# The second layer's modulation: from matmuls beside the first mixer to VectorE multiply-adds beside the dense channel mixer

## The chip, the cores and the metric

The kernel runs on one core of a Trainium2 chip. The metric is the time of one execution in device microseconds (us); the time before is the median of three runs. One more execution was recorded by the hardware profiler. TensorE is called PE, its weight loads PEld, VectorE DVE, ScalarE ACT, GpSimd POOL and SyncE, which issues the DMAs, SP.

## What is computed

Two layers of a hybrid backbone over 256 context and 256 latent tokens of width 1024. Each layer has a token mixer (four head groups between one input and one output projection) and a channel mixer: a dense SwiGLU in layer 0, eight experts with the best two of them in layer 1. Each layer's shifts, scales and gates, its modulation, are six vectors of 1024 for the latent tokens (from c) and six for the context tokens (from c_ctx):

```python
for l in range(DEPTH):                       # DEPTH = 2, D_MODEL = 1024, 256 latent + 256 context tokens
    ctx_out = l < DEPTH - 1
    mod_l = (jax.nn.silu(c) @ ada_w[l] + ada_b[l])[:, None, :]       # ada_w[l]: 1024 x 6144
    mod_c = jax.nn.silu(c_ctx) @ ada_w[l] + ada_b[l]
    sh1, sc1, g1, sh2, sc2, g2 = jnp.split(mod_l, 6, axis=-1)
    csh1, csc1, cg1, csh2, csc2, cg2 = jnp.split(mod_c, 6, axis=-1)
    hl = modulate(rmsnorm(xl, norm_mix[l]), sh1, sc1)
    hc = modulate(rmsnorm(xc, norm_mix[l]), csh1, csc1)
    ...
    yl = jnp.concatenate([ya_l, yb_l, yc_l, yd_l], axis=-1) @ w_out[l]
    xl = xl + g1 * yl
    hl = modulate(rmsnorm(xl, norm_ffn[l]), sh2, sc2)
    if l % 2 == 0:
        xl = xl + g2 * swiglu(hl, ffn_w13[l // 2], ffn_w2[l // 2])
    else:
        xl = xl + g2 * moe_ffn(hl, moe_router[l // 2], moe_router_b[l // 2], moe_w13[l // 2], moe_w2[l // 2])
    if ctx_out:
        ...                                  # the context stream, with cg1, csh2, csc2, cg2
```

In layer 1 the context stream ends with the token mixer, so only sh1 and sc1 are used of its context modulation. All arithmetic is float32; large products are made of a high and a low part of each operand.

## The kernel before

The stages follow one another: setup, layer 0's modulation and first normalisation (`first_h`), the first mixer (`mixer(0, True)`, then `w_out`), normalisation (`make_h`), the dense channel mixer (`ffn`), the second mixer (`mixer(1, False)`), and the experts (`moe`). Within a stage a scheduler at build time orders each engine's instructions by priority and simulated readiness; the order on every engine is fixed when the kernel runs.

**The modulation.** `ada` (line 317) makes 1024 columns of the modulation for both token kinds. The 1024 rows of `ada_w` come in eight loads of 128 x 1024 floats (512 KB, line 335) into four buffers `adaw`. For every second row block, four matmuls (line 347) multiply them by `stat`, whose two used columns are silu(c) and silu(c_ctx): 32-column weights, 512 columns, one quarter of the PSUM bank's partitions each, summed over the row blocks. ScalarE copies the bank to `adar` (line 354), four small matmuls with the constant `sel` (line 358) turn the rows into columns, and DVE adds the bias into `mod[l]` (line 363). For the last group of layer 1 two more matmuls of 512 columns (line 371) and two DVE additions (line 375) spread the channel mixer's gate over all partitions, as `g2row`, which the experts use. There are six groups in a layer. Groups 1 and 0 of layer 0 run alone in `first_h`; the other ten are steps of a generator that runs beside the first mixer.

**Beside.** `beside` (line 378) keeps a generator and a rate, one for each of two phases of the mixer. `tick` (line 388) is called after each block of matmuls of the main work and runs as many steps as the rate says. A step's instructions go behind the latest instruction of the main work on their engine (`issue_after(anchor(...))`). `finish` (line 398) runs what is left. `self.made` is the last DVE instruction of the main work at a tick; DVE instructions of helpers, and the low halves of weights, don't count for it.

**The dense mixer.** `ffn` (line 301) goes through 22 blocks of 128 hidden columns in three parts (8, 8, 6). For each pair of blocks it loads the value and the gate weights (1024 x 256 each, in two loads of 512 KB into three raw buffers), ScalarE makes the high half (line 209), DVE the low half (line 210) of each 128 x 512 piece, and PE makes four banks of 24 matmuls (lines 526 to 528, for the first block 569 to 571). ScalarE takes silu of the gate (line 1323), DVE multiplies (line 1325), ScalarE and DVE split the product (lines 1328, 1329). Then `w2` follows in four quarters with two banks each, and DVE adds the gated result to the residual `xT` (line 1343). The stage's PSUM pool has seven banks A and one bank C; only A is used in it.

## Time and profile before

| | |
|---|---|
| median of three runs | 2014.39 us (2011.48 to 2016.26) |
| profiled execution | 2016.45 us, of which the span from the first to the last instruction is 2014.7 us |
| PE busy | 1876.2 us (93%), mean granted clock 0.962 of full speed |
| PEld, DVE, ACT, POOL busy | 1235.0, 918.4, 767.2, 85.3 us |
| DMA | 474.73 MB, mean 236 GB/s |

The profile is one execution. A busy time counts each moment once in which an engine has an instruction; PE's matmuls are pipelined and their ends are modelled, so neighbouring matmuls overlap in it. A float32 matmul may show as two records. In a timeline, consecutive instructions of one line are merged: the number behind the x counts them. "Idle before" names what ended an engine's idle time. DMA is the mean busy share of the core's 16 DMA engines.

### The profile page before, as it was taken

To read this page: it belongs to the slowest core of one execution; us is meant where nothing else is said; L and a number is where in the kernel's file an instruction comes from. 1 tells how busy PE (TensorE), PEld (TensorE's weight loads), DVE (VectorE), ACT (ScalarE), POOL (GpSimd) and SP (SyncE) were. 2 spreads that over 40 slices of the span, in tenths; PEclk is the share of its full clock that TensorE was granted. 3 is DMA by queue.
4 is the path that set the end of the run, shared out by engine and by line. 5 is a ranking of instruction groups with operands and counts; after the bars stand their busy time and mean duration, and the time that the engine had idled before them with its cause. 6 is when DMAs were issued, how large, how long until landed. Compare 5 with 4: busy or idle time off the path is not lost.

```text
span 2014.7 us, 26293 instructions
## 1 busy us (share of the span) xinstructions
PE 1876.2 (93%) x10051; PEld 1235.0 (61%) x10051; DVE 918.4 (46%) x1678; ACT 767.2 (38%) x1331; POOL 85.3 (4%) x121
## 2 busy tenths in 40 slices
PE   6999999989999999888988999789999989899988
PEld 3777455678888888667686886454454444444443
DVE  3556334453433434675567965333324333333323
ACT  3745433253223233654547854232322222323221
POOL 0210111000000000210100000000000000000000
PEclk8999899989999999888998989999999989999999
DMA  8543356412323233331045969999999989999997
GB/s 276 181 136 110 126 193 204 152 63 95 96 93 96 92 97 92 102 85 48 1 166 201 363 225 380 405 408 409 401 376 349 410 321 380 409 401 372 409 405 300
DMA packets 190958, 474.73 MB, mean 236 GB/s; under 512 B 18596, under 2 KB 81768, under 8 KB 190824
## 3 DMA queue, kind: packets, MB, share of 16 engines
q1 hardware_dynamic: 190456, 472.76, 64.2%
q8 instruction: 81, 1.33, 0.3%
q14 instruction: 53, 0.43, 0.1%
q10 hardware_dynamic: 368, 0.21, 0.0%
HBM read 471.88 MB, written 1.05 MB: 235 GB/s over the span
## 4 chain that ended last, share of the span: by engine, by line
PE 63%; DMA 5%; DVE 5%; ACT 3%; issue 2%; DVEq 0%; SPq 0%; ACTq 0%
PE bankA L1572 16%; PE bankA L528 7%; PE bankA L527 7%; PE bankA L526 7%; PE bankA L1567 6%; PE bankA L1568 5%; PE bankA L1566 5%; DMA w<-in_moe_w_dram 5%; DVE wl L210 2%; ACT wh L209 1%; PE bankA L1531 1%; PE bankA L1602 1%; PE bankA L835 1%; PE bankB L874 1%; PE bankA L1714 1%
## 5 line engine op out<-in xcount | busy, mean ns | idle before, releaser
L210 DVE TENSOR_TENSOR wl<-w,wh 128x1024 fp32r<-128x1024 f32 x222 | 263.9, 1222 | 257.8 <-ACT wh L209 245.7
L209 ACT ACTIVATE wh<-w 128x1024 fp32r<-128x1024 f32 x222 | 225.7, 1053 | 156.7 <-DMA w<-in_moe_w_dram 126.7
L1572 PE MATMUL bankA<-w,xl 128*32 128x256 f32 (+3 forms) x1784 | 228.4, 452 | 15.0 <-DMA w<-in_moe_w_dram 15.0
L1572 PEld LDWEIGHTS bankA<-w,xl 128*32 128x32 f32 (+1 forms) x1784 | 83.7, 124 | 134.3 <-issue 96.5
L1567 PE MATMUL bankA<-wl,xe 128*128 128x512 f32 x336 | 140.7, 419 | 19.2 <-DVE wl L210 19.2
L1566 PE MATMUL bankA<-wh,xe 128*128 128x512 f32 x336 | 129.0, 425 | 14.8 <-ACT wh L209 14.4
L1568 PE MATMUL bankA<-wh,xe 128*128 128x512 f32 x336 | 136.5, 406 | 0.0
L1572 PE MATMUL bankA<-w,ut 128*32 128x256 f32 (+1 forms) x792 | 116.4, 490 | 0.8 <-DMA w<-in_moe_w_dram 0.8
L1650 ACT ACTIVATE sg<-bankA 128x512 f32<-128x512 f32 (+2 forms) x45 | 23.1, 533 | 196.6 <-PE bankA L1572 159.1
L1566 PEld LDWEIGHTS bankA<-wh,xe 128*128 128x128 f32 x336 | 61.7, 194 | 54.4 <-ACT wh L209 28.8
L1567 PEld LDWEIGHTS bankA<-wl,xe 128*128 128x128 f32 x336 | 65.9, 196 | 44.0 <-DVE wl L210 29.7
L1567 PE MATMUL bankA<-wl,uh 128*128 128x512 f32 x168 | 68.8, 409 | 9.4 <-DVE wl L210 9.4
L1653 DVE TENSOR_TENSOR sg<-bankA,sg 128x512 f32<-128x512 f32 (+2 forms) x45 | 27.0, 612 | 108.7 <-PE bankA L1572 89.0
L1572 PEld LDWEIGHTS bankA<-w,ut 128*32 128x32 f32 (+1 forms) x792 | 36.6, 122 | 63.9 <-issue 56.5
L1568 PEld LDWEIGHTS bankA<-wh,xe 128*128 128x128 f32 x336 | 66.0, 196 | 13.9
L528 PE MATMUL bankA<-uh,w2l 128*128 128x512 f32 x176 | 70.2, 399 | 0.0
L528 PE MATMUL bankA<-hh,wgl 128*128 128x512 f32 x176 | 70.2, 399 | 0.0
L527 PE MATMUL bankA<-hl,wgh 128*128 128x512 f32 x176 | 69.3, 394 | 0.0
L527 PE MATMUL bankA<-ul,w2h 128*128 128x512 f32 x176 | 69.3, 394 | 0.0
L526 PE MATMUL bankA<-uh,w2h 128*128 128x512 f32 x176 | 69.0, 392 | 0.0
L526 PE MATMUL bankA<-hh,wgh 128*128 128x512 f32 x176 | 69.0, 392 | 0.0
L347 PE MATMUL bankC<-adaw,stat 128*32 128x512 f32 x352 | 67.3, 617 | 1.5 <-DMA adaw<-in_ada_w_dram 1.5
(489 smaller groups left out, 3679.1 us busy)
## 6 DMA issues: line engine op xcount, KB each, us to landing
w<-in_moe_w_dram SPq DMA_DIRECT2D x286, 1024.0 KB, 10.1
adaw<-in_ada_w_dram SPq DMA_DIRECT2D x96, 512.0 KB, 4.8
xT<-in_moe_w_dram SPq DMA_DIRECT2D x47, 1024.0 KB, 9.2
wa<-in_ffn_w_dram SPq DMA_DIRECT2D x22, 512.0 KB
wg<-in_ffn_w_dram SPq DMA_DIRECT2D x22, 512.0 KB, 3.5
w<-in_ffn_w_dram SPq DMA_DIRECT2D x20, 512.0 KB, 3.4
wo<-in_w_out_dram SPq DMA_DIRECT2D x12, 512.0 KB, 3.5
wU<-in_w_in_dram SPq DMA_DIRECT2D x4, 512.0 KB
```

The costliest lines, as they stand in the source:

```text
L209: nc.scalar.activation(h, src, AF.Copy)
L210: ins = nc.vector.tensor_tensor(lo[:, q:q + m], src, h.bitcast(F32), op=OP.subtract)
L347: mark(nc.tensor.matmul(b[32 * q:32 * q + 32], lhsT=self.stat[:, j], rhs=rs[j][:, h * 512:(h + 1) * 512], start=(i == 1), stop=(i == 7)))
L526: t.matmul(out, lhsT=whi, rhs=hhi, start=start, stop=False)
L527: t.matmul(out, lhsT=whi, rhs=hlo, start=False, stop=False)
L528: t.matmul(out, lhsT=wlo, rhs=hhi, start=False, stop=stop)
L1566: t.matmul(b, lhsT=x[0], rhs=hi[:, c], start=start, stop=False)
L1567: t.matmul(b, lhsT=x[0], rhs=lo[:, c], start=False, stop=False)
L1568: t.matmul(b, lhsT=x[1], rhs=hi[:, c], start=False, stop=stop)
L1572: t.matmul(out[0][n * s:n * s + n, 0:h], lhsT=x, rhs=w[:, s * h:(s + 1) * h], start=start, stop=stop)
L1650: nc.scalar.activation(g[:, 0:h], b[:, 0:h], AF.Silu)
L1653: V.tensor_tensor(g[:, 0:h], b[:, 0:h], g[:, 0:h], op=OP.mult)
```

## The change

Layer 1's six groups leave the generator beside the first mixer. Layer 0's four remaining groups keep it, with matmuls in batches of eight instead of four, a lag of one step instead of three, and half the rate. A new generator, `ada_vec`, makes layer 1's modulation beside the dense mixer, in twelve units of 512 columns. A unit loads eight blocks of 128 x 512 (256 KB each) into six buffers; DVE multiplies the first block by silu(c), one scalar for each partition, and adds the seven others times their scalars (`scalar_tensor_tensor`); units 0 to 3 do so for c and c_ctx, the others for c alone. DVE then transposes the sum in blocks of 32 x 32 and sums the 32 columns of each block; four matmuls with a new constant `fold` (four stacked 32 x 32 identities) add the four partition groups into a bank C, and DVE adds the bias. For the last two units one matmul of 512 columns with `ones` each spreads the gate for `g2row`. `ffn` gets ticks after its gate and value banks (24 matmuls each) and, at 0.7, after its w2 banks. The setup keeps silu(c) in a tile `sl` of its own.

```diff
--- before.py
+++ after.py
@@ -33,7 +33,7 @@
 BEYOND = ((0, 160, 128), (1, 128, 128), (2, 64, 128), (3, 64, 64), (4, 64, 64), (5, 64, 64), (6, 32, 64), (7, 128, 128))
 
 CONST_COLS = {
-    "base": [("ident", 128), ("ones", 128), ("sel", 4)],
+    "base": [("ident", 128), ("ones", 128), ("sel", 4), ("fold", 32)],
     "mix": [("mask_f", 128), ("mask_b", 128), ("swa_m0", 128), ("swa_m1", 128), ("sel_i", 64), ("sel_f", 64)],
     "rope": [("mla_c", 128), ("mla_s", 128), ("swa_c", 256), ("swa_s", 256)],
     "moe": [("utri", 128), ("iota", 320), ("idx8", 8), ("rev8", 8), ("tri8", 64)],
@@ -85,6 +85,7 @@
         put(n + "_c", cs)
         put(n + "_s", sn)
 
+    put("fold", np.tile(np.eye(32), (4, 1)))
     put("sel", np.stack([(p % 32 == m) & (p // 32 % 2 == h) for h in range(2) for m in range(2)], 1))
     si, sf = np.zeros((128, 64)), np.zeros((128, 64))
     for h in range(4):
@@ -237,14 +238,14 @@
 
         b = self.bank()
         nc.tensor.transpose(b[:, 0:16], p0, self.ident[0:16, 0:16])
-        sl = self.mp.tile([128, 16], F32, name="sl")
+        sl = self.sl = self.cp.tile([128, 16], F32, name="sl")
         self.stat = self.mp.tile([128, 8, 32], F32, name="stat")
         nc.gpsimd.memset(self.stat, 0.0)
         nc.scalar.activation(sl, b[:, 0:16], AF.Exp, scale=-1.0)
         nc.vector.tensor_scalar(sl, sl, 1.0, None, op0=OP.add)
         nc.vector.reciprocal(sl, sl)
-        nc.vector.tensor_tensor(self.stat[:, :, 0:2], sl.rearrange("p (s k) -> p k s", s=2),
-                                b[:, 0:16].rearrange("p (s k) -> p k s", s=2), op=OP.mult)
+        nc.vector.tensor_tensor(sl, sl, b[:, 0:16], op=OP.mult)
+        nc.vector.tensor_copy(self.stat[:, :, 0:2], sl.rearrange("p (s k) -> p k s", s=2))
         self.p2 = self.T2("p2", shape=(128, 128))
         nc.gpsimd.memset(self.p2, 1.0)
         self.load_x()
@@ -338,14 +339,15 @@
             if not lag:
                 load(k)
             i = k - lag
-            if i > 0 and i % 2:
-                if i == 1:
+            if i > 0 and i % 4 == 3 or not lag and i % 2:
+                if b is None:
                     b = self.bank(tag)
                 with own(nc.tensor):
-                    for q in range(4):
-                        j, h = i - 1 + q // 2, q % 2
-                        mark(nc.tensor.matmul(b[32 * q:32 * q + 32], lhsT=self.stat[:, j], rhs=rs[j][:, h * 512:(h + 1) * 512],
-                                              start=(i == 1), stop=(i == 7)))
+                    for f in range(i // 4 * 4 if lag else i - 1, i, 2):
+                        for q in range(4):
+                            j, h = f + q // 2, q % 2
+                            mark(nc.tensor.matmul(b[32 * q:32 * q + 32], lhsT=self.stat[:, j],
+                                                  rhs=rs[j][:, h * 512:(h + 1) * 512], start=(f == 0), stop=(f == 6)))
             if lag and k < 8:
                 load(k)
             yield
@@ -364,16 +366,57 @@
                                          b[:, 0:16].rearrange("p (j h m) -> p j h m", h=2, m=2),
                                          self.pc1[:, o:o + 8].rearrange("p (h j) -> p j h", h=2).unsqueeze(3)
                                          .to_broadcast([128, 4, 2, 2]), op=OP.add))
-        if l == 1 and g == 5:
-
-            for h in range(2):
-                with own(nc.tensor):
-                    mark(nc.tensor.matmul(b, lhsT=self.C("sel")[:, 2 * h:2 * h + 1].to_broadcast([128, 128]), rhs=row,
-                                          start=True, stop=True))
-                s = self.g2row[:, h * 512:(h + 1) * 512]
-                with own(nc.vector):
-                    mark(nc.vector.tensor_tensor(s, b, s, op=OP.add))
-        yield
+        yield
+
+    def ada_vec(self, l, n, mk, segs=(0, 1), lag=0):
+
+
+        nc = self.nc
+        acc = [mk("adaacc") if m in segs else None for m in range(2)]
+        src = self.I["ada_w"][l, :, n * 512:(n + 1) * 512].rearrange("(k p) c -> p k c", p=128)
+        for k in range(8):
+            r = mk("adav")
+            with self.tc.issue_after(self.anchor(nc.sync)):
+                ins = nc.sync.dma_start(r, src[:, k])
+            self.aside.add(ins.ins.name)
+            for m in segs:
+                sc = self.sl[:, 8 * m + k:8 * m + k + 1]
+                a = acc[m]
+                with self.tc.issue_after(self.made):
+                    if k:
+                        ins = nc.vector.scalar_tensor_tensor(a, r, sc, a, op0=OP.mult, op1=OP.add)
+                    else:
+                        ins = nc.vector.tensor_scalar(a, r, sc, None, op0=OP.mult)
+                    self.aside.add(ins.ins.name)
+            yield
+        for _ in range(lag):
+            yield
+
+        m0, ns = segs[0], len(segs)
+        sm = mk("adasum", (128, 32))[:, 0:16 * ns].rearrange("p (m c) -> p m c", m=ns)
+        for i, m in enumerate(segs):
+            t = mk("adat")
+            with self.tc.issue_after(self.made):
+                a = nc.vector.transpose(t, acc[m])
+                b = nc.vector.tensor_reduce(sm[:, i], t.rearrange("p (b c) -> p b c", c=32), axis=AX.X, op=OP.add)
+                self.aside |= {a.ins.name, b.ins.name}
+        for _ in range(lag):
+            yield
+        last = self.anchor(nc.tensor)
+        o = l * 64 + 16 + 4 * n
+        with self.tc.issue_after(last):
+            b = self.bank("C")
+            sv = sm.rearrange("p m (j q) -> p q m j", q=4)
+            for q in range(4):
+                nc.tensor.matmul(b[32 * q:32 * q + 32, 0:4 * ns], lhsT=self.C("fold"), rhs=sv[:, q], start=True, stop=True)
+            nc.vector.tensor_tensor(self.mod[l][:, 4 * n:4 * n + 4, m0:m0 + ns],
+                                    b[:, 0:4 * ns].rearrange("p (m j) -> p j m", m=ns),
+                                    self.pc1[:, o:o + 4].unsqueeze(2).to_broadcast([128, 4, ns]), op=OP.add)
+            if l == 1 and n >= 10:
+                b = self.bank("C")
+                nc.tensor.matmul(b, lhsT=self.C("ones"), rhs=acc[0], start=True, stop=True)
+                s = self.g2row[:, (n - 10) * 512:(n - 9) * 512]
+                nc.vector.tensor_tensor(s, b, s, op=OP.add)
 
     def beside(self, gen, rate):
 
@@ -1318,6 +1361,7 @@
                         for k in range(KD):
                             self.mm3(b, hi[:, k, s], lo[:, k, s], self.hh[k], self.hl[k], k == 0, k == KD - 1)
                         bs.append(b)
+                        self.tick()
                 for j in range(2):
                     sg = fp.tile([128, NT], F32, name="sg", tag="sg", bufs=2)
                     nc.scalar.activation(sg, bs[2 + j], AF.Silu)
@@ -1344,6 +1388,7 @@
                                                        self.xT[m][:, c], op0=OP.mult, op1=OP.add)
                     if f0 == 16:
                         self.square_x(m)
+                    self.tick(0.7)
 
 
     U2 = 22
@@ -1822,8 +1867,7 @@
                 def mk(nm, sh):
                     return self.mp.tile(list(sh), F32, name=nm, tag=nm, bufs={"adaw": 4, "adar": 1}[nm])
 
-                todo = [(0, g) for g in (2, 3, 4, 5)] + [(1, g) for g in range(6)]
-                self.beside(overlap([self.ada(l, g, mk, lag=3) for l, g in todo], 10), (1.2, 2.4))
+                self.beside(overlap([self.ada(0, g, mk, lag=1) for g in (2, 3, 4, 5)], 10), (0.6, 1.2))
                 self.mixer(0, True)
                 self.ahead = 0
                 self.w_out(0, True)
@@ -1832,7 +1876,11 @@
             self.scale_mod(0, 1)
             with pool(name="ffn0", bufs=1) as fp, pool(name="ffn0s", bufs=1) as self.mp, self.psum("pffn", A=7, C=1):
                 self.make_h(0, 1, self.ffn_h(fp))
+                mk = lambda nm, sh=(128, NT): fp.tile(list(sh), F32, name=nm, tag=nm,
+                                                      bufs={"adaacc": 6, "adav": 6, "adat": 3, "adasum": 2}[nm])
+                self.beside(overlap([self.ada_vec(1, n, mk, (0, 1) if n < 4 else (0,), lag=2) for n in range(12)], 8), 1.8)
                 self.ffn(0, fp)
+                self.finish()
                 self.scale_mod(1, 0)
                 self.scale_mod(1, 1, 1)
             with pool(name="y1", **right) as yp, self.psum("pmix1", A=4, B=4):
```

## Rows read from the trace of the kernel before

**Rows 1.** The page, part 1: busy time of PE over the span.
```profile
PE 1876.2 (93%) x10051; PEld 1235.0 (61%) x10051; DVE 918.4 (46%) x1678; ACT 767.2 (38%) x1331; POOL 85.3 (4%) x121
```

**Rows 2.** The chain that ended last: start us, us, what.
```profile
427.04 2.93 PE bankA L422 x16
...
810.38 1.93 PE bankA L422 x16
```

**Rows 3.** The table of stretches: the stretch, its length, then as its head says.
```profile
core 0: us, PE busy (x) PEld busy (x) DVE busy (x) ACT busy (x) POOL busy (x), PEclk, DMA share, GB/s
...
43.00:427.00 384.00, 374.61 (x1937) 241.02 (x1937) 189.28 (x476) 166.31 (x372) 46.02 (x64) 0.97 0.48 153
...
262.00:391.00 129.00, 129.00 (x718) 69.90 (x718) 51.18 (x159) 37.95 (x113) 13.46 (x22) 1.00 0.59 193
...
445.00:534.00 89.00, 89.00 (x383) 71.31 (x382) 34.56 (x53) 32.08 (x53) 0.00 (x0) 1.00 0.30 95
445.00:800.00 355.00, 355.00 (x1523) 285.32 (x1522) 139.72 (x223) 111.96 (x186) 0.00 (x0) 1.00 0.30 92
830.00:1040.00 210.00, 193.66 (x1140) 151.85 (x1139) 132.02 (x339) 111.03 (x244) 35.55 (x44) 0.93 0.21 60
970.00:1030.00 60.00, 60.00 (x397) 46.47 (x396) 32.24 (x110) 23.62 (x71) 10.14 (x16) 1.00 0.00 1
```

**Rows 4.** Timeline of PE, 262 to 275 us: start us, us, engine, line, operation.
```profile
264.98 1.06 PE L347 MATMUL bankC<-adaw,stat 128*32 128x512 f32 x8
265.97 0.66 PE L860 MATMUL bankA<-c_base,P 128*128 128x128 f32 x4
...
270.68 1.05 PE L347 MATMUL bankC<-adaw,stat 128*32 128x512 f32 x4
271.66 0.44 PE L860 MATMUL bankA<-c_base,P 128*128 128x128 f32 x2
```

**Rows 5.** Groups by line, 262 to 391 us: operation, count, busy us, mean ns, idle before.
```profile
L347 PE MATMUL bankC<-adaw,stat 128*32 128x512 f32 x192 | 37.0, 604 | 0.0
...
L358 PE MATMUL bankC<-c_base,adar 128*128 128x4 f32 x48 | 6.0, 248 | 0.0
...
L371 PE MATMUL bankC<-adar,c_base 128*128 128x512 f32 x4 | 2.2, 624 | 0.0
```

**Rows 6.** Table of stretches for line 347 alone: PE, PEld, clock, DMA share, GB/s.
```profile
214.00:262.00 48.00, 13.53 (x64) 1.83 (x64) 0.91 0.51 168
```

**Rows 7.** Timelines of weight loads (PEld): one modulation group, one old fold.
```profile
264.98 0.16 PEld L347 LDWEIGHTS bankC<-adaw,stat 128*32 128x32 f32 x8
...
279.97 0.97 PEld L358 LDWEIGHTS bankC<-c_base,adar 128*128 128x128 f32 x8
```

**Rows 8.** Groups of DVE by line and shape, whole span: count, busy us, mean ns.
```profile
L842 DVE TENSOR_REDUCE nm<-bankA 128x1 f32<-128x512 f32 x32 | 22.1, 691 | 34.7 <-PE bankA L835 18.9 <-PE bankA L838 15.4 <-POOL P L854 0.4
...
L1068 DVE SCALAR_TENSOR_TENSOR uc<-uT,pc,uc 128x510 f32<-128x510 f32 x8 | 5.6, 742 | 0.0
...
L1065 DVE TENSOR_SCALAR uc<-uT,pc 128x512 f32<-128x512 f32 x4 | 2.3, 612 | 0.0
```

**Rows 9.** Timeline of DVE, 61 to 66 us: four multiply-adds in a row.
```profile
62.96 2.73 DVE L1068 SCALAR_TENSOR_TENSOR uc<-uT,pc,uc 128x510 f32<-128x510 f32 x4
```

**Rows 10.** Timelines of DVE and PE in the dense mixer, at the step to w2.
```profile
529.22 0.69 DVE L210 TENSOR_TENSOR w2l<-w,w2h 128x512 fp32r<-128x512 f32 x1 [0.72 <-ACT w2h L209]
...
528.99 0.40 PE L528 MATMUL bankA<-uh,w2l 128*128 128x512 f32 x1
...
533.19 0.40 PE L528 MATMUL bankA<-uh,w2l 128*128 128x512 f32 x1
```

**Rows 11.** Waits of SP's queue, 430 to 810 us: us in total, times, longest us.
```profile
SPq L182 <- DVE w2l L210: 113.7, 24, 8.0
```

**Rows 12.** DMA issues, whole span: count, KB each, median us to landing.
```profile
wg<-in_ffn_w_dram SPq DMA_DIRECT2D x22, 512.0 KB, 3.5
...
wo<-in_w_out_dram SPq DMA_DIRECT2D x8, 256.0 KB, 3.2
```

## The prediction

> **What bounds the kernel now.** I read the page first: over the whole span TensorE (PE) is busy 93% [rows 1], so the first question is whether that busy time is real work in the two stages the change touches. The chain of work that ended last gives the edges of the stages: the sums for the two norms that follow the first mixer and the dense channel mixer stand at 427 and 810 us [rows 2]. I then cut the span with the table of stretches [rows 3]. The first mixer runs from 43 to 427 us, the dense mixer from about 445 to 809, the second mixer to about 1040, the experts to the end. In the first mixer PE is idle 384 - 374.6 = 9.4 us, and in its stretch from 262 to 391 not at all, while VectorE (DVE) is busy 40% of that stretch and ScalarE 29%. In the dense mixer PE is busy all of the 355 us read there and DVE 39%. So PE sets the pace on both sides of the move, and DVE has room on average where the work is going. The experts' stage does not read a clock of its own: it starts when the second mixer ends, so what is gained before 810 us moves the end by as much.
>
> Third, PE's timeline inside the stretch from 262 to 391 [rows 4]. A group of four modulation matmuls (8 records) starts at 264.98 and the next instruction at 265.97: it holds PE for 0.99 us. Split in two (4 records each) either half also holds it for 0.98 us (270.68 to 271.66). These durations repeat, so they are occupation and not hidden waiting.
>
> **What it removes from the first mixer.** All of layer 1's modulation lies between 262 and 391 us. Its busy time by groups of instructions [rows 5]: 37.0 us in the weighted sums (192 records are 24 groups of four; at about 1.05 a piece that is 35 pieces, so 11 groups were issued as two halves), 6.0 us in the 48 records that fold the rows into columns, 2.2 us in the two broadcasts for g2row; together 45.2 us. A piece reads 0.07 longer than it holds PE (270.68 + 1.05 against 271.66), 3 us over 43 pieces; I keep 45.2 and leave that to the range. The six ScalarE copies, the DVE additions and 48 loads of 512 KB go as well; none of these ends a PE wait today, so they count as nothing here.
>
> At this place a rule speaks against the change. The table of stretches has weight loads (PEld) busy 69.9 of 129 us, 54%, between 262 and 391, and 285 of 355, 80%, in the dense mixer [rows 3]. The Trainium skill, "Perfetto Trace Analysis", section "Identifying the Most-Contended Engine", says that matmul busy time is a poor measure for TensorE and that weight-load busy time and arithmetic share show its headroom. By it the stretch would have headroom in which the 45 us lay free of charge, and the sum would begin with 0 instead of -45. I do not take it: the starts in [rows 4] show the next matmul pushed back by the whole piece.
>
> **Layer 0's four groups.** They stay on PE, at half the rate and in batches of eight matmuls. Between 214 and 262 us 64 records, eight groups of four, took 13.5 us [rows 6]; eight whole pieces at 1.05 would be 8.4, and one piece there ran at a lowered clock (the stretch's mean is 0.91), so about four were split, 4 us. Batches can save between 0 and 4.2 us; I take 3. Their 42 steps at half the rate last as long as 84 of the old 104, so they still end before the output projection ends, so nothing waits for them.
>
> **What it adds to PE in the dense mixer.** Twelve folds, each four matmuls on 32-column weights with at most 8 columns, and two broadcasts of 512 columns. No such fold is in the trace. Upper bound: the old fold, the same count with 128-column weights, 6.0 / 6 = 1.0 us each [rows 5], so 12.0. Lower: weights of 32 columns load eight in 0.16 us where the old fold's eight take 0.97 [rows 7], and one record of the old fold lasts 0.248, so 0.41 each, 4.9. I take 0.6, as the loads are those of the cheap kind and the rest that of the dear: 7.2. The broadcasts have the shape of those removed: 2.2. In a stage with no idle PE none of it is hidden: +9.4 (7.1 to 14.2). A fold also waits for its unit's reduction, with the dense matmuls queued behind it on PE; it is emitted two steps later (2 / 1.8 ticks, one for each 24 matmuls, some 6 us), and costs nothing more while DVE is late by less than that.
>
> **What it adds to DVE.** Twelve units of eight steps; four of them for two rows (c and c_ctx), eight for one: 112 multiply-adds, 16 first products, 16 block transposes, 16 reductions. The same multiply-add (two SBUF operands, a scalar per partition, 510 columns, accumulating on itself) has a mean of 0.742 [rows 8], and four in a row take 2.73, 0.68 each [rows 9]: I use 0.70. A tensor-scalar is 0.612 and a reduction over 512 columns 0.691 [rows 8]; a transpose has no row, I give it the reduction's 0.69 (an estimate). 112 x 0.70 + 16 x 0.61 + 32 x 0.69 = 78.4 + 9.8 + 22.1 = 110 us. DVE then has 140 + 110 = 250 of 355 us, 70%. The average hides the tight place: the two-row units come first. From 445 to 534 us (four pairs of gate and value, 16 ticks, 16 x 1.8 = 28.8 steps, 3.6 units of 13.8 us) DVE's 34.6 [rows 3] becomes 84 of 89 us, 95%. What hides it is the slack of the weight splits: the low half finished at 529.22 + 0.69 = 529.91 is first used at 533.19 [rows 10], 3.3 us later. DVE runs in order, so behind a late multiply-add wait the split of the weights, and behind that PE; and at the change from gate/value to w2 the last uh/ul. I charge 3 us of PE waiting for it (0, when DVE stays within its slack, to 10, when multiply-adds take 0.9 instead of 0.70 in that block: 3.6 x 14 x 0.2).
>
> **Queues.** 25.2 MB move from the first mixer to the dense one, as 96 loads of 256 KB: 71 GB/s on top of 92 in 355 us, where the DMA share is 0.30; the first mixer carries 153 at 0.48 today [rows 3], so no limit is near. On SP the weight loads now stand behind loads that wait for a multiply-add to free one of six buffers. Weight loads already wait there for their split, up to 8.0 us at a time [rows 11], and land in 3.5 us, a 256 KB load in 3.2 [rows 12]; 18 matmuls lie between 528.99 and 533.19 [rows 10], 0.233 us each, so one weight block of 48 lasts 11.2 us on PE, and some 7 us of lateness is free (an estimate, 11.2 less a landing). Cost 0; if that cover is gone, it is the slower rival below. Nothing of the change is issued on POOL. The setup gets one more copy of 128x16 on DVE and 16 KB more of constants: a fraction of a microsecond, counted 0.
>
> **The end of the stage.** The steps needed are 11 x 8 + 13 = 101. The dense mixer has 44 ticks in its gate/value part and 24 x 0.7 = 16.8 in w2, 60.8 x 1.8 = 109 steps. So the last fold falls in the last w2 block, some 25 us before its end, and nothing is left to the final drain: cost 0.
>
> **Gaps that open.** With the fillers gone, chains of softmax (scores, maximum, exponential, transposes) may leave PE waiting. The second mixer has the same attention without any filler, and from 970 to 1030 us PE is busy all 60 of 60 [rows 3]. So 0 is the near bound; I take 3, and 17 at the far end (first rival).
>
> **Sum.** -45.2 - 3 + 9.4 + 3 + 3 = -32.8 us. The profiled execution took 2016.45 (span 2014.7), 2.06 over the median of the three, 2014.39. Against that median: 1981.5.
>
> **Rivals.** (1) Softmax chains take over in part. The second mixer as a whole has 210 - 193.7 = 16.3 us of idle PE, 7.8% [rows 3]; the same share of the 339 us left of the first mixer is 26, 17 more than today's 9.4. For it: it is the same code without fillers. Against: the second mixer's idle time lies ahead of its attention, the removed work inside it. -32.8 + 14 = -18.8: 1995.6. (2) The chains set the pace wholly and the fillers were free: 0 from the mixer, +9.4 and +3 in the dense stage, +12.4: 2026.8. The starts in [rows 4] speak against. It is where the rule of the Trainium skill, "Perfetto Trace Analysis", on weight-load busy time leads. (3) The slower side, by queueing: a multiply-add at the head of DVE waits for its load, the loads come six at a time, and 96 loads are 16 turns. If in each turn DVE stands 3 us beyond the 3.3 us of slack, PE loses 48: 1981.5 - 3 + 48 = 2026.5. It turns slower from 2.2 us a turn on (35.8 / 16). For it: one in-order SP queue with waiting loads, and a DVE at 95% early. Against: 3.2 us of landing with six buffers, which last 6 x 1.4 = 8.4 us in two-row units and 4.2 in one-row units. (4) The change does not do what it says: the steps are not done when the stage ends. At ten steps too few, some 1.4 us each on DVE plus a landing, about +17: 1998.5.
>
> **How the numbers follow.** Forecast 75%, with 1968 to 1996 as its own range (best: -45.2 - 4.2 + 7.1 = -42.3, 1972; worst: -45.2 + 3 for the overlap + 14.2 + 3 of gaps + 10 = -15 would need every bound at once, -18 is taken, 1996; below, some 4 us for the spread of the runs, 2011.5 to 2016.3). Rival 1: 11%, rival 2: 3%, rival 3: 8%, rival 4: 3%. To leave out no more than 2 in 10 the range runs from 1968 to 2003, with rivals 1 and 4 inside. Faster by over 0.2% (4 us, about what a measurement can tell from no change): the forecast, rivals 1 and 4 less a tail, 0.86. Slower: rivals 2 and 3, 0.10. Between: 0.04.
>
> **What would show it.** Right: the first mixer ends some 45 us earlier with PE still over 95% busy; the dense stage is some 12 us longer, with PE busy and DVE at 70%; folds of about 0.6 us; the later stages as long as before. Wrong: PE waits on ScalarE or DVE in the attention (rivals 1, 2); PE waits on a DVE split, or DVE on a load of ada_w, in the dense stage (rival 3); multiply-adds after the last w2 block (rival 4).

## The result and the profile after

The changed kernel takes 1984.62 us (median of 4 runs, 1976.54 to 1996.20) against 2013.59 for the kernel before (2011.48 to 2016.26) on the same chip: a ratio of 0.9844, 95% interval 0.9816 to 0.9871. In a second comparison it took 1985.75 (6 runs) against 2016.12: 0.9847 (0.9808 to 0.9887). (The ratios in this document are those on record; they are not the quotients of the two medians and differ from these by up to 0.0034.) The profiled execution took 1978.8 us, 37.65 less than the profiled one of before. The forecast was 1981.5. The executions of one kernel differ by more than I had allowed: twelve of the changed kernel lie between 1974.38 and 1996.20 with a median of 1982.2, and the mean granted clock falls steadily along them, from 0.963 to 0.950. Seven of the twelve lie between 1974 and 1983 us and five between 1988 and 1997; of the four runs of the first comparison two lie in either part. The kernel before spreads as far (2006.08 to 2032.51 in 23 runs of one comparison). So the stages below are read from several profiled executions.

The page of the changed kernel, part 1: busy time and share of the span for each engine.

```profile
PE 1831.2 (93%) x9907; PEld 1224.3 (62%) x9907; DVE 1014.5 (51%) x1845; ACT 763.5 (39%) x1325; POOL 86.6 (4%) x121
```

PE has lost 45.0 us of busy time [rows 1] and its share is the 93% it was; DVE has gained 96.1. The chain that ended last (start us, us, what) has the norms' sums, now under line 465:

```profile
385.12 2.19 PE bankA L465 x16
...
773.01 1.93 PE bankA L465 x16
...
1018.66 1.96 PE bankA L465 x8
```

Against [rows 2] the first norm comes 41.9 us earlier and the second 37.4. Here are the stages of all profiled executions of both kernels, cut at the first matmul of the mixer's input projection and at these three norms; e9 is the kernel before once more, e1, e10 and e11 are the changed kernel (see the experiments).

| us | to the mixer | first mixer | dense | second mixer | experts to the end |
|---|---|---|---|---|---|
| before | 44.24 | 382.80 | 383.34 | 245.52 | 958.80 |
| before (e9) | 42.20 | 386.27 | 381.77 | 244.60 | 958.76 |
| after | 45.61 | 339.51 | 387.89 | 245.65 | 958.24 |
| after (e1) | 43.35 | 339.63 | 387.85 | 244.91 | 965.36 |
| after (e10) | 45.07 | 340.42 | 387.85 | 245.02 | 958.54 |
| after (e11) | 47.73 | 339.70 | 387.88 | 245.22 | 959.17 |

By the means of the rows, the first mixer is 384.5 - 339.8 = 44.7 us shorter, the dense stage 387.9 - 382.6 = 5.3 us longer, and the time to the mixer 2.2 longer (it varies by more than that from run to run). Sum: -37.2 us at the second norm. The 383.34 of the first profile of before is 1.6 us above e9's 381.77 because of its first 17 us, where the granted clock was 0.57 (0.68 in e9); against 381.77 the dense stage is 6.1 us longer. The second mixer is as long as it was, and so are the experts but for one execution.

The table of stretches of the changed kernel (columns as in [rows 3]): the first mixer, the transition, the first 89 us of the dense stage, and 355 us of it.

```profile
43.00:385.00 342.00, 326.08 (x1694) 231.78 (x1693) 186.51 (x469) 163.42 (x367) 47.41 (x64) 0.96 0.31 98
385.00:403.00 18.00, 13.66 (x58) 11.24 (x59) 11.95 (x31) 14.60 (x34) 0.00 (x0) 0.72 0.34 116
403.00:492.00 89.00, 89.00 (x402) 70.55 (x401) 74.83 (x122) 30.74 (x50) 0.00 (x0) 1.00 0.52 175
403.00:758.00 355.00, 355.00 (x1596) 281.63 (x1595) 235.71 (x391) 108.60 (x179) 0.00 (x0) 1.00 0.48 159
```

In the mixer PE's idle time grew from 9.4 us [rows 3] to 342 - 326.1 = 15.9. Part of that lies ahead of the mixer: from its first matmul to the norm it grew from 382.80 - 374.62 = 8.2 to 339.51 - 326.00 = 13.5. In the dense stage PE is busy all of 355 us, at full clock, with DVE at 74.8 of 89 (84%) and 235.7 of 355 (66%). DMA went from 92 to 159 GB/s there, 0.48 of the engines' time.

Groups of instructions of the dense stage, 403 to 775 us: the work that DVE took over.

```profile
L387 DVE SCALAR_TENSOR_TENSOR adaacc<-adav,sl,adaacc 128x512 f32<-128x512 f32 x112 | 79.7, 743 | 2.3 <-DMA adav<-in_ada_w_dram 2.1
...
L400 DVE STREAM_TRANSPOSE adat<-adaacc 128x512 f32<-128x512 f32 x16 | 11.3, 704 | 0.0
L401 DVE TENSOR_REDUCE adasum<-adat 128x16 f32<-128x512 f32 x16 | 10.9, 678 | 0.0
L389 DVE TENSOR_SCALAR adaacc<-adav,sl 128x512 f32<-128x512 f32 x16 | 7.4, 480 | 0.0
```

The four DVE groups add up to 109.3 us, beside 110 forecast. DVE waited 2.1 us in all for the data. What PE pays is read from the starts of its matmuls. PE's timeline around a fold (line 411) and around a broadcast (line 417):

```profile
439.99 0.39 PE L571 MATMUL bankA<-hh,wgl 128*128 128x512 f32 x1
440.31 0.25 PE L411 MATMUL bankC<-adasum,c_base 128*32 128x8 f32 x8
440.49 0.50 PE L569 MATMUL bankA<-hh,wah 128*128 128x512 f32 x1
440.83 0.39 PE L570 MATMUL bankA<-hl,wah 128*128 128x512 f32 x1
441.06 0.40 PE L571 MATMUL bankA<-hh,wal 128*128 128x512 f32 x1
...
746.70 0.39 PE L570 MATMUL bankA<-ul,w2h 128*128 128x512 f32 x1
746.93 1.05 PE L417 MATMUL bankC<-adaacc,c_base 128*128 128x512 f32 x2
747.42 0.80 PE L571 MATMUL bankA<-uh,w2l 128*128 128x512 f32 x1
748.05 0.40 PE L569 MATMUL bankA<-uh,w2h 128*128 128x512 f32 x1
```

The dense matmuls start every 0.233 us. From 439.99 to 441.06 three of them pass: 1.07 - 0.70 = 0.37 us for the fold (the twelve folds read 0.35 to 0.38 in this way). From 746.70 to 748.05 two pass: 1.35 - 0.47 = 0.88 for the broadcast. 12 x 0.37 + 2 x 0.88 = 6.2 us. That is the whole lengthening of the stage (+6.1 against experiment e2, which has no modulation in it).

PE's waits in the first mixer (what waits <- for what: us in total, times, longest); between 403 and 758 us the same view has no row at all.

```profile
PE bankA L878 <- ACT P L892: 3.0, 2, 1.7
PE bankA L612 <- ACT hh L479: 2.5, 1, 2.5
PE bankA L626 <- DVE wSkl L211: 2.3, 1, 2.3
PE bankB L712 <- DVE bb L707: 2.2, 1, 2.2
PE bankA L1264 <- ACT sc L1261: 1.6, 1, 1.6
```

The wait on a weight split (`wSkl`) is new, those on the attention's exponentials (3.0 beside 1.7), on `bb` and on `sc` have grown: the gaps that fillers used to hide. No single chain has taken over. Last, the waits of SP's queue from 385 to 775 us:

```profile
SPq L183 <- DVE w2l L211: 98.6, 20, 8.3
...
SPq L380 <- DVE adaacc L387: 25.1, 21, 2.9
...
SPq L380 <- DVE adaacc L389: 4.8, 1, 4.8
```

The new loads hold SP for at most 4.8 us each time, less than the weight loads hold it already [rows 11].

### The profile page after: what moved, and what is told of

Same layout as the page of the kernel before. It is cut to its first block, busy times and chain, and to the rows that moved or that the text cites. A ratio compares the mean times of both kernels' runs of the same rounds, so it can differ in the third digit from the quotient of the medians.

```text
span 1976.9 us, 26253 instructions
## 1 busy us (share of the span) xinstructions
PE 1831.2 (93%) x9907; PEld 1224.3 (62%) x9907; DVE 1014.5 (51%) x1845; ACT 763.5 (39%) x1325; POOL 86.6 (4%) x121
## 4 chain that ended last, share of the span: by engine, by line
PE 64%; DVE 5%; DMA 5%; ACT 3%; issue 2%; DVEq 0%; SPq 0%; ACTq 0%
PE bankA L1617 16%; PE bankA L569 7%; PE bankA L571 7%; PE bankA L570 7%; PE bankA L1612 6%; PE bankA L1613 5%; PE bankA L1611 5%; DMA w<-in_moe_w_dram 5%; DVE wl L211 3%; ACT wh L210 1%; PE bankA L1576 1%; PE bankA L1647 1%; PE bankA L878 1%; PE bankB L917 1%; PE bankA L1759 1%
## 5 line engine op out<-in xcount | busy, mean ns | idle before, releaser
L1612 PEld LDWEIGHTS bankA<-wl,xe 128*128 128x128 f32 x336 | 65.9, 196 | 44.7 <-DVE wl L211 30.6
L387 DVE SCALAR_TENSOR_TENSOR adaacc<-adav,sl,adaacc 128x512 f32<-128x512 f32 x112 | 79.7, 743 | 2.3 <-DMA adav<-in_ada_w_dram 2.1
```

What stands on the lines that cost most here:

```text
L387: ins = nc.vector.scalar_tensor_tensor(a, r, sc, a, op0=OP.mult, op1=OP.add)
L1612: t.matmul(b, lhsT=x[0], rhs=lo[:, c], start=False, stop=False)
```

## The experiments

Each kernel is the changed one with the edit shown, unless said otherwise. Stage times are cut as in the table above.

**e1, e10, e11: the changed kernel again** (no edit); **e9: the kernel before again** (no edit).

> The changed kernel once more, unchanged, for the spread of its times (1976.5, 1978.8, 1990.4, 1996.2 so far, with mean granted clocks 0.962, 0.960, 0.953, 0.950). Theory A, the sum holds and the higher times are stretches at the lower clock that come in some executions only: times again between 1976 and 1997, falling with the clock, and a profile of a high one shows the added time in a stage that the change does not touch or in mixer gaps at a lower clock. Theory B, the dense stage sometimes stalls on VectorE: a profile of a high one shows PE waits on DVE L211 or on adav there, 10 us and more.

> The changed kernel, a third profile. From the start of the first mixer to the first norm 338 to 341, to the second norm 387 to 389 in every execution; if its time is near 1990, the surplus lies behind the second norm, in the second mixer or the experts (245 and 958 to 965 so far), at a lower clock. If it lies in the dense stage with PE waiting on DVE, the change itself has an unsteady cost.

> As e10, a fourth profile of the changed kernel: same numbers expected.

> The kernel before, profiled a second time, for the part of a time that has nothing to do with the change. The stages beside the change should be as in the first profile within 3 us (start of the first mixer 43 to 46 us, from there to the first norm 382 to 385, to the second 383, to the third 245), and what its time differs by from 2016 should lie in the experts (958.8 us from the third norm to the end there).

Measured: 1985.75 us (six runs, 1974.38 to 1993.55), and in the single runs 1978.66 and 1981.47; e9 2015.42. Their stages stand in the table. The four dense stages agree within 0.04 us and the four mixers within 0.9; the kernel before varies by 3.5 in its mixer. The other experiments show a wider spread. e2, e4, e6 and e7 run the same work on PE in the same order in the first mixer, and with them eight executions of it take 336.3 to 340.4 us, the two shortest (e4, e6) at a mean granted clock of 0.97, the two longest (e2, e10) at 0.95. The first 17 us of the dense stage differ by up to 1.6 (see e7). So a difference of 2 us in one of these stages can be told from single profiles only where its place in the stage is known.

None of the four profiled executions of the changed kernel took 1988 us or more, but e7 (1988.72) and e6 (1995.09) did. Their edits do not touch the second mixer, and it takes 256.25 and 254.70 us there, beside 244.9 to 245.7 in the four. In e7 against the changed kernel the surplus comes in one stretch, 150 to 180 us after the second norm. The changed kernel, then e7:

```profile
923.00:953.00 30.00, 29.92 (x178) 20.85 (x177) 16.80 (x54) 17.09 (x54) 6.61 (x10) 1.00 0.00 1
```

```profile
921.00:951.00 30.00, 29.91 (x116) 20.43 (x114) 11.34 (x36) 12.37 (x38) 5.29 (x8) 0.66 0.00 1
```

PE is as busy in both, but the granted clock is 0.66 instead of 1.00, and PE gets through 116 matmul records instead of 178. e6 reads the same there (0.66). In the 30 us ahead all three read alike (PE busy 23.4 us, clock 0.72), so what decides was not seen. The 7 us that e1 lost in the experts lie near their start: 10 us at 0.54 (1035.74 to 1045.74) where the changed kernel has 1.00.

**e2: without layer 1's modulation.** The parts of the change are the removal from the mixer and the addition to the dense stage; this is the removal alone. The vectors keep the bias only, which alters which experts are chosen and sends the last stage down another branch (2933.78 us), so it is read up to the third norm.

```diff
+        nc.vector.tensor_copy(self.mod[1], self.pc1[:, 80:128].unsqueeze(2).to_broadcast([128, 48, 2]))
...
-                self.beside(overlap([self.ada_vec(1, n, mk, (0, 1) if n < 4 else (0,), lag=2) for n in range(12)], 8), 1.8)
```

> Removal alone: layer 1's modulation is left out in both places, its values are the bias only, so routing and output differ; stages up to the second mixer have the same work otherwise. My sum: first mixer as in the changed kernel (norm at about 385 us against 427), dense stage without the added work. If the addition costs what I charged (9.4 on PE, 3 of waiting), the dense stage is 12 us shorter than in the changed kernel (387.8, so 375); by the matmul starts of the changed kernel's trace (0.38 a fold, 0.88 a broadcast, no waits) it is 6.3 shorter (381.5).

Measured, from the chain of e2:

```profile
385.08 2.00 PE bankA L466 x16
...
766.84 1.93 PE bankA L466 x16
```

The mixer takes 340.43 us, as in the changed kernel, the dense stage 766.84 - 385.08 = 381.76, as in e9 (381.77). The whole gain of the mixer is therefore there without any modulation of layer 1 (layer 0's new batches and rate, which e2 keeps, included), and the change costs the dense stage 387.87 - 381.76 = 6.1 us.

**e3: the addition alone.** The mixer keeps all ten groups as before, and the dense stage makes layer 1's modulation a second time, into a tile that nobody reads.

(Also undone in it, not shown: the batches of eight; the `g2row` matmuls are back in the mixer.)

```diff
+        self.mod2 = cp.tile([128, 48, 2], F32, name="mod2")
...
-            nc.vector.tensor_tensor(self.mod[l][:, 4 * n:4 * n + 4, m0:m0 + ns],
+            nc.vector.tensor_tensor(self.mod2[:, 4 * n:4 * n + 4, m0:m0 + ns],
...
-                self.beside(overlap([self.ada(0, g, mk, lag=1) for g in (2, 3, 4, 5)], 10), (0.6, 1.2))
+                todo = [(0, g) for g in (2, 3, 4, 5)] + [(1, g) for g in range(6)]
+                self.beside(overlap([self.ada(l, g, mk, lag=3) for l, g in todo], 10), (1.2, 2.4))
```

> Addition alone: the first mixer as before (layer 1 on PE in groups of four matmuls, lag 3, old rates), and the twelve units beside the dense mixer as well, their results into scratch. My sum: dense stage +9.4 and up to +3 of waiting, 2014 + 9 to 12 = 2023 to 2026. By the starts in the changed kernel's trace: +6.3, 2020. If the earlier start or higher clock of the changed kernel hid the cost, up to 2030. First norm at 427 as before in all of them.

Measured: 2024.73 against 2016.12 us as medians (10 and 23 runs), ratio 1.0033 (1.0002 to 1.0065). The mixer is back at 384.09, the dense stage is 389.99: 6.7 over the profile of before, 8.2 over e9. That is up to 2 more than in the changed kernel; 1 us of it comes in the first 10 us of its dense matmuls, where the granted clock was 0.73 instead of 0.84. The other builds up evenly: its dense matmuls start every 0.2343 us on average, beside 0.2333 in the changed kernel; why was not found. PE waits for nothing in the 355 us that follow.

**e4: the place without the engine.** Layer 1's groups stay on PE but move beside the dense stage. (Not shown: `stat` is kept for longer, and the `g2row` matmuls are back in `ada`.)

```diff
...
-                self.beside(overlap([self.ada_vec(1, n, mk, (0, 1) if n < 4 else (0,), lag=2) for n in range(12)], 8), 1.8)
+                mkp = lambda nm, sh: fp.tile(list(sh), F32, name=nm, tag=nm, bufs={"adaw": 5, "adar": 1}[nm])
+                self.beside(overlap([self.ada(1, g, mkp, lag=1) for g in range(6)], 12), 1.4)
```

> Place without engine: layer 1's six groups stay matmuls on PE, in batches of eight, and run beside the dense mixer instead of the first mixer; layer 0 as in the changed kernel. If the gain is the change of engine (PE full in both stages, my reading), the first mixer gains its 42 and the dense stage pays 24 whole pieces of 0.99 to 35 of them, six folds of 1.0 and 2.2: +32 to +45, so 2004 to 2017. If the gain is the change of place (fillers free in the dense stage, costly in the attention), 1975 to 1985.

Measured: 2001.08 us (1999.42 to 2022.49) against 2016.12, ratio 0.9959 (0.9929 to 0.9989). The dense stage is 414.88 us, 33.1 more than e2's (1.2 of it in its first 17 us, at a granted clock of 0.57). Its groups on PE, 380 to 795 us:

```profile
L349 PE MATMUL bankC<-adaw,stat 128*32 128x512 f32 x192 | 23.1, 598 | 0.0
...
L360 PE MATMUL bankC<-c_base,adar 128*128 128x4 f32 x48 | 5.7, 242 | 0.0
...
L373 PE MATMUL bankC<-adar,c_base 128*128 128x512 f32 x4 | 2.1, 618 | 0.0
```

23.1 + 5.7 + 2.1 = 30.9 us of matmuls make the stage 33.1 us longer: beside dense matmuls this work hides nowhere. The same 192 records took 37.0 in the mixer [rows 5]: there they stood in 35 pieces, here in twelve of 16 records, two whole groups each, that hold PE for 1.85 us. So the place is worth a part (the second norm comes at 794.59, 16 us before that of the kernel before), and the engine the rest: 33.1 us on PE became 6.1.

**e5: batches and lag alone.** All ten groups on PE beside the mixer at the old rates, with the new batches of eight and a lag of 1; no `ada_vec`. (Not shown: the `g2row` matmuls are back in `ada`.)

```diff
...
-                self.beside(overlap([self.ada(0, g, mk, lag=1) for g in (2, 3, 4, 5)], 10), (0.6, 1.2))
+                todo = [(0, g) for g in (2, 3, 4, 5)] + [(1, g) for g in range(6)]
+                self.beside(overlap([self.ada(l, g, mk, lag=1) for l, g in todo], 10), (1.2, 2.4))
...
-                self.beside(overlap([self.ada_vec(1, n, mk, (0, 1) if n < 4 else (0,), lag=2) for n in range(12)], 8), 1.8)
```

> Batches alone: all ten groups stay on PE beside the first mixer at the old rates, but in batches of eight matmuls with a lag of one step. If split groups cost a whole piece each (my reading of the 0.98 us halves), the 11 splits of layer 1 and 4 of layer 0 go, some 15 us: first mixer 383 to 368, time near 2001. If the halves only fill time that would be idle otherwise, or if a batch now waits for its last load (landing in 4.6 to 6.4 us), 0 to -4: 2012 to 2016.

Measured: 2016.42 us against 2018.99, ratio 0.9994 (0.9956 to 1.0032). The group of the weighted sums, 43 to 431 us:

```profile
L349 PE MATMUL bankC<-adaw,stat 128*32 128x512 f32 x320 | 64.1, 631 | 0.0
```

PE's timeline, line 349, from 262 us:

```profile
265.21 1.05 PE L349 MATMUL bankC<-adaw,stat 128*32 128x512 f32 x4
267.25 1.05 PE L349 MATMUL bankC<-adaw,stat 128*32 128x512 f32 x4
```

The same group of before reads 59.0 us from 43 to 427. The 40 groups of eight records stand in 51 pieces (55 before), and 38 of these are halves of four records, such as the two shown: at the old rates the batches did not keep the groups together. Batches alone therefore do not give the saving at layer 0.

**e6: each multiply-add twice** (the second into a tile that is not read).

```diff
+        dum = mk("adat")
...
                         ins = nc.vector.scalar_tensor_tensor(a, r, sc, a, op0=OP.mult, op1=OP.add)
+                        self.aside.add(ins.ins.name)
+                        ins = nc.vector.scalar_tensor_tensor(dum, r, sc, a, op0=OP.mult, op1=OP.add)
```

> Slack of DVE: each multiply-add of the twelve units runs twice (the second into scratch), 224 instead of 112. DVE would have 236 + 80 = 316 of 355 us, and in the first 89 us (74.8 measured) 74.8 + 37 to 45 = 112 to 120. If DVE's slack is what hides the work, and 84% in the first block is near its end, PE waits in the dense stage and it is 25 to 35 us longer (413 to 423 instead of 388). If PE is hardly touched by DVE at all (the scheduler moves the multiply-adds behind the splits, and later blocks take them up), under 10 us longer.

Measured: one execution, 1995.09 us; dense 397.49, 9.6 more than in the changed kernel. Its first 89 and its 355 us in the table of stretches:

```profile
400.00:489.00 89.00, 89.00 (x396) 70.74 (x395) 85.33 (x136) 30.29 (x51) 0.00 (x0) 1.00 0.49 156
400.00:755.00 355.00, 350.14 (x1562) 276.33 (x1561) 305.06 (x495) 106.15 (x174) 0.00 (x0) 0.99 0.48 157
```

PE's waits, 400 to 768 us:

```profile
PE bankA L573 <- DVE ul L1376: 4.2, 1, 4.2
PE bankA L572 <- ACT uh L1375: 0.6, 1, 0.6
```

Another 69 us on DVE bring it to 86% of the 355 us and 96% of the tight block, and PE first waits where the prediction put it, on the last `ul` at the change to w2, once, for 4.2 us (509.9 to 514.5). Behind that wait the matmuls start 0.43 us apart instead of 0.233 until 522.2, at a granted clock of 0.55 from 515 to 520. Wait and clock together make 8.2 of the 9.6 us at this one place; the other 1.4 come in the first 17 us of the stage, as in e7, where no multiply-add was doubled. At the change's own 66% this slack is not touched.

**e7: each fold twice.**

```diff
+            for q in range(4):
+                nc.tensor.matmul(b[32 * q:32 * q + 32, 64:64 + 4 * ns], lhsT=self.C("fold"), rhs=sv[:, q], start=True, stop=True)
```

> Price of a fold: each of the twelve folds runs twice, the second into unused columns. My prediction's 0.6 us a fold: dense stage +7.2. By the starts in the changed kernel's trace (0.27 for the fold and 0.1 for the matmul behind it): +3.2 to +4.5.

Measured: one execution, 1988.72 us; dense 390.12, 2.25 more. Most of that is not the folds. The first 16 us of the stage, ahead of any fold, in the changed kernel and then in e7:

```profile
385.00:401.00 16.00, 11.66 (x49) 9.65 (x50) 10.00 (x27) 12.73 (x31) 0.00 (x0) 0.68 0.38 131
```

```profile
381.00:397.00 16.00, 11.78 (x44) 9.82 (x44) 9.10 (x26) 11.38 (x28) 0.00 (x0) 0.57 0.36 125
```

At the lower clock e7 is 1.4 us behind before its first fold starts, and twelve second folds share the other 0.8: 0.07 each. PE's timeline around the first of them says the same:

```profile
436.98 0.39 PE L573 MATMUL bankA<-hh,wgl 128*128 128x512 f32 x1
437.30 0.25 PE L411 MATMUL bankC<-adasum,c_base 128*32 128x8 f32 x8
437.38 0.23 PE L413 MATMUL bankC<-adasum,c_base 128*32 128x8 f32 x8
437.54 0.50 PE L571 MATMUL bankA<-hh,wah 128*128 128x512 f32 x1
437.87 0.39 PE L572 MATMUL bankA<-hl,wah 128*128 128x512 f32 x1
```

From the fold's start to the next dense matmul 0.24 us pass, beside 0.18 in the changed kernel (440.31 to 440.49). The second folds stand right behind the first ones, so 0.07 is the price of four more such matmuls and not of the interruption: some 0.3 of a fold's 0.37 us go with breaking into the stream of dense matmuls.

**e8: the rest of the modulation to DVE as well.** Layer 0's four groups beside the first mixer are made by `ada_vec` too, with three load buffers instead of six.

```diff
...
-                self.beside(overlap([self.ada(0, g, mk, lag=1) for g in (2, 3, 4, 5)], 10), (0.6, 1.2))
+                mk0 = lambda nm, sh=(128, NT): self.mp.tile(list(sh), F32, name=nm, tag=nm,
+                                                            bufs={"adaacc": 4, "adav": 3, "adat": 1, "adasum": 2}[nm])
+                self.beside(overlap([self.ada_vec(0, n, mk0, (0, 1), lag=2) for n in range(4, 12)], 8), (1.0, 2.0))
```

> One step further: layer 0's four groups beside the first mixer become eight two-row units on DVE as well. PE gives up 16 pieces of 1.05 and four folds of 0.95, gets 8 x 0.38: -17. DVE in the first mixer goes from 187 of 342 us to 187 + 8 x 13.4 = 294 (86%). If a full PE sets the pace there and DVE's room is free as in the dense stage: 1968 (first norm near 367). If the mixer's DVE work stands in the softmax chains, so that multiply-adds ahead of it hold PE: first norm later than 385, PE waits on DVE or on ScalarE behind it, 1990 to 2015.

Measured: 2040.58 us against 2018.99, ratio 1.0076 (1.0044 to 1.0108); the profiled execution is the slowest of its runs (2049.14). The mixer takes 391.07 us, 51 more. A stretch of it:

```profile
200.00:380.00 180.00, 152.58 (x632) 92.56 (x631) 131.51 (x315) 58.00 (x177) 25.86 (x35) 0.71 0.21 65
```

The longest waits of PE and ScalarE, 43 to 430 us:

```profile
PE bankA L878 <- ACT P L892: 18.1, 10, 3.1
...
ACT P L892 <- DVE nm L890: 41.5, 8, 11.4
ACT P L892 <- DVE nm L887: 32.9, 8, 11.8
```

DVE is busy 131.5 of 180 us, 73%, not much more than the 66% that cost nothing in the dense stage. Here its queue carries the softmax's maxima and reciprocals (`nm`): ScalarE's exponentials wait 74 us for them (39 in the changed kernel), PE waits for the exponentials, and with PE idle for 15% of the stretch the granted clock falls to 0.71 of full speed, between the levels of 2.4 and 1.2 GHz; in the changed kernel PE is idle 2% of the same 180 us and the clock is 0.96. DVE's own waits for the loads are small (5.1 us in the whole span), so the fewer buffers do not explain it. Over the whole mixer PE's idle time grows from 13.5 to 391.07 - 349.56 = 41.5 us, and its busy time from 326.0 to 349.56 although some 17 us of work, by the expectation's count, have left: so the lower clock (0.84 over the mixer, beside 0.96) costs at least as much as the waits.

**e12: the last group of layer 0 to the dense stage.** Only g2 of layer 0 (group 5), which the dense mixer needs at its first w2 block, leaves the mixer; it is the first thing that `ada_vec` makes.

```diff
-                self.beside(overlap([self.ada(0, g, mk, lag=1) for g in (2, 3, 4, 5)], 10), (0.6, 1.2))
+                self.beside(overlap([self.ada(0, g, mk, lag=1) for g in (2, 3, 4)], 10), (0.6, 1.2))
...
-                self.beside(overlap([self.ada_vec(1, n, mk, (0, 1) if n < 4 else (0,), lag=2) for n in range(12)], 8), 1.8)
+                todo = [(0, 10, (0, 1)), (0, 11, (0, 1))] + [(1, n, (0, 1) if n < 4 else (0,)) for n in range(12)]
+                self.beside(overlap([self.ada_vec(l, n, mk, m, lag=2) for l, n, m in todo], 8), 2.0)
```

> A version that may beat both: layer 0's last group (the dense mixer's own gate, first needed at its w2) also leaves PE and becomes the first two units on DVE beside the dense mixer; 14 units at a rate of 2.0. PE gives up four pieces of 1.05 and a fold of 0.95 and gets two folds of 0.38: first mixer -5, dense stage +0.8, so 4 us under the changed kernel, by stage lengths more than by time. If the early two-row work is too much for DVE (six two-row units instead of four, 84% in the first block already) or the gate comes late for w2, the dense stage is 3 to 15 us longer and the sum the same or slower.

Measured: 1976.39 us (four runs, 1969.73 to 1986.16) against 2015.61, ratio 0.9815 (0.9780 to 0.9850). The mixer is 332.56, 7 shorter than in the changed kernel, the dense stage 388.56, 0.7 longer (two folds of 0.37), with no wait of PE between 393 and 748 us:

```profile
393.00:748.00 355.00, 355.00 (x1605) 281.81 (x1604) 259.17 (x432) 109.21 (x180) 0.00 (x0) 1.00 0.53 171
```

DVE is at 73% of the dense stage, as in e8's stretch, and PE still waits for nothing: it is what stands behind the added work on DVE that decides, not the share. The intervals of this ratio and of the changed kernel's overlap; what speaks for a gain is the mixer. Of its 7 us some 3 can be the spread, as e4 and e6, with layer 0's four groups still in it, read 336.3; it is 3.7 below these, less the 0.7 of the dense stage. A gain of some 3 us is thus likely, but the times do not show it.

## Why the prediction was right, and where its steps were off

**What bounds.** PE set the pace on both sides, as read from [rows 3]. The decisive reading was that of the starts in [rows 4]: a piece of modulation holds PE for 0.98 us. 45.2 us of such work went, and the mixer became 44.7 shorter (e2, without the addition, has the same mixer). Rival 2, that the fillers were free, falls with that. The rule of the Trainium skill that led there ("Perfetto Trace Analysis", "Identifying the Most-Contended Engine": judge TensorE's headroom by its arithmetic share and its weight-load busy share), read as room for more work free of charge, does not agree with this trace: weight loads were at 54% of that stretch, and the work in it cost its full time.

**The mixer's terms.** Forecast -45.2 - 3 + 3. At layer 0 the weighted sums fell from 59.0 - 37.0 = 22.0 to 16.8 us (128 records, in 11 pieces instead of 20, six of them of 16 records) and the folds from 10.8 - 6.0 = 4.8 to 4.1, together -5.9, beyond my bound of 4.2; the gaps came to +5.3 (8.2 to 13.5) instead of +3. Two errors of 2 to 3 us cancelled, and that the mixer's sum held is partly luck. With -45.2 for layer 1 the sum is -45.8, where the stage table has -44.7 by its means and -43.3 between the first two profiles: PE's busy time in the mixer fell by 374.62 - 326.00 = 48.6 us between these and not by 51.1. The difference, 2.5, is near the 3 us by which the pieces read longer than they hold PE, named in the prediction and left to its range. The reason I gave for layer 0, the batches, holds only in part: with half the steps six pieces of 16 records came out whole, and in e4 all twelve of layer 1, but at the old rates the batches fell apart again (e5). The half rate with batches of four was not tested.

**Rival 1,** the softmax chains: of the 17 us that it allowed, 5.3 came. PE is busy 95% of the mixer, as the forecast's test had it.

**The dense stage.** Forecast +9.4 for folds and broadcasts and +3 for waits, measured +6.1 and no wait. A fold was the mis-sized term: 0.37 us, not 0.6, and below my lower bound of 0.41, which had added the weight loads (0.16) to a whole record of the old fold (0.248). By the starts the eight records hold PE for 0.18 us in all (440.31 to 440.49), and the rest is the wider spacing of the dense matmuls on either side (0.32 and 0.34 instead of 0.233), which my sum did not have. The broadcasts cost 1.8 (2.2 forecast).

**DVE.** 109.3 us of work (110 forecast): the multiply-adds 0.71 each by their group (0.70), the transposes 0.704 (0.69 estimated), the reductions 0.678 (0.69), the first products 0.48 (0.61). DVE's union grew by 96 us, so it stood at 66% and 84%, not 70% and 95%. The slack in [rows 10] held: e6 had to double the multiply-adds before PE waited, and then at the place named.

**Queues and the end of the stage.** Rival 3 did not come: the loads landed in 4.0 us, DVE waited 2.1 us for them in all, SP 4.8 at most at a time. The last fold starts at 744.78, 28 us before the second norm (some 25 before the end forecast), so rival 4 fell too.

**The total.** The profiles give -37.2 us at the second norm where -32.8 was forecast; the difference is the dense stage's 12.4 that was 5.3 to 6.1, less the 2 us of a later start of the mixer. The medians show 29 to 30 us. Of the four runs of the changed kernel two (1976.54, 1978.80) lie 35 to 37 us under the median before, as the stages say, and two (1990.43, 1996.20) 17 to 23; executions that long were seen to lose time at a lower granted clock behind the second norm (e6, e7), where the change moves nothing. So the total came within 3 us partly by luck: the stages gained 4.4 us more than forecast, and the median of these four runs gave that back. The range, 1968 to 2003, was wide enough for all twelve runs.

## What to carry to other kernels

Where an engine sets the pace, read an instruction's price from the starts of its neighbours, not from its busy time or from a share: this gave 0.98 us for a group that went and 0.37 us for a fold that came. A stage's length in one execution can mislead too: in e7 it grew by 0.19 us for each second fold, where the starts show 0.07. Work moves well to an engine with room when what stands behind it there has slack (weight splits, 3.3 us ahead of their use); the same engine at much the same load cost 51 us in a stage where the softmax's short chain runs through it (e8). Small fillers can hide gaps as well as cost time, so charge some of the removed time back (here 5.3 of some 50 us).

## What the runs showed of the hardware that was not expected

- A `scalar_tensor_tensor` of 128 x 512 floats took 0.743 us (mean of 112), 0.68 when six ran in a row (4.06 us); a `tensor_scalar` with one operation 0.480, where the one of before with two took 0.612 [rows 8].
- Four 32-column matmuls of 4 or 8 columns cost 0.37 us in a stream of 512-column matmuls, and four more right behind them 0.07 (e7): most of the price is the break in the stream.
- The mean granted clock differs from one execution to the next and the time with it, in both kernels: 0.963 with 1974.38 us and 0.950 with 1996.20 after the change, 0.966 with 2006.08 and 0.955 with 2032.51 before. In e6 and e7 a single stretch of 30 us at 0.66 instead of 1.00, with PE as busy, goes with a second mixer 9 to 11 us longer.
